# HGRN score levels in column strips, mLSTM products by head on array halves, and one conv tap moved to ScalarE

## The chip, the core and the metric

The kernel runs on one core of one Trainium2 chip. The metric is the device time of one execution in microseconds (us): the median of several runs. Beside these runs one execution is recorded by the hardware profiler; all rows of traces come from that one.

## What is computed

A decoder layer on 512 tokens of width 1024, in float32. Two half-step SwiGLU feed-forward blocks stand around a token mixer; each of the three has an RMS norm before and after it. The mixer has two groups of heads that read columns of one projection:

```python
# HGRN2, 4 heads of 128: S_t = diag(f_t) S_{t-1} + k_t v_t^T, o_t = S_t^T q_t
scores = jnp.sum(qc[:, :, :, None, :] * kc[:, :, None, :, :] * decay, axis=-1)   # decay = exp(G_t - G_s), s <= t
o = o_inter + jnp.einsum("bhts,bhsv->bhtv", scores, vc)
# mLSTM, 4 heads, q and k of 64, v of 128
num = inter[..., None] * jnp.einsum("bhtd,bhdv->bhtv", qc, C) + jnp.einsum("bhts,bhsv->bhtv", P, vc)
C_new = keep[..., None, None] * C + jnp.einsum("bhs,bhsd,bhsv->bhdv", w, kc, vc)
# q and k of the mLSTM go through a causal depthwise convolution of width 4
qk = jax.nn.silu(causal_depthwise_conv(jnp.concatenate([mq, mk], axis=-1), conv_w, conv_b))
```

## The kernel before

Everything lies in SBUF; weights stream from HBM. A weight tile is split into a high and a low float32r part (a copy on ScalarE, L208, and a subtraction on VectorE, L210), and a product is three matmuls: high by high, high by low, low by high. TensorE does these nearly all the time. The first feed-forward block comes first, the mixer's projections at L433 run from 364.4 us on, and after 600 us the second block follows. Inside the mixer the small products of the recurrences are plain float32; the trace shows each of these as two matmul records in a row on the same operands (112 matmuls at L1057 make 224 records).

**How the order is made.** Each engine runs its own program in order. The Tile framework places the instructions; the kernel steers TensorE by hand with `fill(n)`: the projections of the mixer (hq, conv, rows, hi, mv, hg, mo) wait in a queue of jobs cut into pieces, and `fill(n)` issues n pieces. A piece of hq or conv is 6 matmuls of 256 columns at L433; a piece of hi, mv, hg or mo is 3 of 512 columns (L126 to L128, called mm3 from here on). Stages of the recurrences stand between fills, so that TensorE works on projections while VectorE and ScalarE prepare the next stage. The four numbers in `FILL` are the pieces per step of the first HGRN pair of heads, the second pair, the mLSTM outputs and the HGRN outputs. The jobs are the same in number whatever FILL says; FILL moves them earlier or later.

**HGRN levels** (`hgrn_levels`, `hgrn_level`, `put`). The scores of a chunk of 128 tokens are built by levels. At level c a block of 2c tokens is halved; the first c tokens are keys, the second c are queries, and the decay goes by the boundary between them. VectorE forms the exponents (L1044, L1045), ScalarE takes exp (L1046, L1047), VectorE multiplies by q (L1049), TensorE forms the scores in one PSUM bank (L1057), and `put` copies the wanted blocks into `sT`. There are two passes (p = 0, 1), each for two heads, that is 8 tiles m of 128 keys by 64 queries, and the levels 64, 32, 16, 8, 4, 2. Before the change level 64 is 8 matmuls of 64 keys by 64 queries, level 32 is 16 of 32 by 32 in the key strips that begin at partitions 0 and 64, and levels 16 to 2 are 8 matmuls each of all 128 keys by 64 queries, from which `put` takes the valid parts with a mask on VectorE (L1030). The bursts of one level stand between fills of 6 pieces (p = 0) or 5 (p = 1). `ke` has two buffers.

**Convolution** (`conv`). ScalarE copies the projection out of PSUM (L1192), VectorE forms the last tap with the bias (L1195) and adds the three others (L1198), for four blocks, in the first pass of levels.

**mLSTM states** (`mlstm_scores`, L1287). For three chunks c and two pairs p of heads, one matmul makes keys (128 columns: two heads of 64) by values (258 columns: two heads of 129); only the two diagonal blocks are used (L1295, L1297). **mLSTM outputs** (`mlstm_values`). For each chunk and pair one bank takes query by state (L1332, 258 columns, from the second chunk on) and score by value for each head (L1335, 129 columns). ScalarE squares them (L1340), VectorE and GpSimd form the norm, and VectorE writes the scaled result (L1354), which frees the bank. `chunks` runs the three stages of four chunks in a staggered way with `fill(2)` between the steps. There are 8 PSUM banks.

Of the kernel before, what the change touches and what calls it, by code (L numbers as in the profile page):

```python
# [10 lines left out]
AF = mybir.ActivationFunctionType  # L11
ALU = mybir.AluOpType
PSUM = bass.MemoryType.PSUM

P = 128
# [8 lines left out]
PAIRS = NF // 2  # L24
HALF = T // 2
KH = ND // 2
FILL = (6, 5, 2, 2)
NH = 4
W = 512
HQ, HF, HI, HG, MQ, MV, MO, MG = 0, 512, 1024, 1536, 2048, 2560, 3072, 3584  # L30
# [37 lines left out]
class Layer:  # L68
# [950 lines left out]
    def put(self, p, n, sc):  # L1019

        c = LEVELS[n]
        so = self.sT[:, 8 * p : 8 * p + 8, :].rearrange("p n (b two c) -> p n b two c", two=2, c=c)[:, :, :, 1, :]
        if c >= 32:
            sc3 = sc.rearrange("p (n b c) -> p n b c", n=8, c=c)
            for b in range(64 // c):
                r = slice(2 * c * b, 2 * c * b + c)
                self.nc.scalar.copy(so[r, :, b], sc3[r, :, b])
            return
        mk = self.mask[:, n : n + 1, :].broadcast_to([P, 8, 64]).rearrange("p n (b c) -> p n b c", c=c)
        self.nc.vector.copy_predicated(so, mk, sc.rearrange("p (n b c) -> p n b c", n=8, c=c))  # L1030

    def hgrn_level(self, p, n, ke):

        nc = self.nc
        c = LEVELS[n]
        q, kk, G = self.q[p], self.kk[p], self.G[p]
        flat = lambda t: t.rearrange("p a t -> p (a t)")
        blk = lambda t: flat(t).rearrange("p (b two c) -> p b two c", two=2, c=c)
        qe = self.st("qe")
        qe3 = qe.rearrange("p (b c) -> p b c", c=c)  # L1040
        el = self.st("el")
        el3 = el.rearrange("p (b c) -> p b c", c=c)
        ref = blk(G)[:, :, 0, c - 1 : c].broadcast_to([P, 512 // c, c])
        nc.vector.tensor_tensor(qe3, blk(G)[:, :, 1, :], ref, op=ALU.subtract)  # L1044
        nc.vector.tensor_tensor(el3, ref, blk(kk)[:, :, 0, :], op=ALU.subtract)  # L1045
        nc.scalar.activation(qe, qe, AF.Exp)  # L1046
        nc.scalar.activation(blk(ke)[:, :, 0, :], el3, AF.Exp)  # L1047
        yield
        nc.vector.tensor_tensor(qe3, qe3, blk(q)[:, :, 1, :], op=ALU.mult)  # L1049
        yield  # L1050
        sc = self.ps()
        k8, q8 = flat(ke).rearrange("p (n s) -> p n s", s=P), qe.rearrange("p (n u) -> p n u", u=64)
        for m in range(8):
            for b in range(1 if c < 32 else 64 // c):
                r = slice(2 * c * b, 2 * c * b + c) if c >= 32 else slice(0, P)
                u = slice(c * b, c * b + c) if c >= 32 else slice(0, 64)
                nc.tensor.matmul(  # L1057
                    sc[r, 64 * m + u.start : 64 * m + u.stop], k8[:, m, r], q8[:, m, u], start=True, stop=True,
                    skip_group_check=True,
                )  # L1060
        yield
        self.put(p, n, sc)
        yield
# [124 lines left out]
    def conv(self, n, ps):  # L1188

        nc = self.nc  # L1190
        x = self.st("cx")
        nc.scalar.copy(x, ps)  # L1192
        tap = lambda j: self.prm[:, 4 * j + n : 4 * j + n + 1]
        y = self.qk[:, n, :]
        nc.vector.tensor_scalar(y, x, tap(3), self.prm[:, 16 + n : 17 + n], op0=ALU.mult, op1=ALU.add)  # L1195
        for j in range(3):
            s = 3 - j
            nc.vector.scalar_tensor_tensor(y[:, s:], x[:, : T - s], tap(j), y[:, s:], op0=ALU.mult, op1=ALU.add)  # L1198
# [30 lines left out]
    def mlstm_scores(self, mc):  # L1229

        nc = self.nc
# [52 lines left out]
        for c in range(3):  # L1284
            for p in range(2):
                ps = self.ps()
                nc.tensor.matmul(  # L1287
                    ps[:, :258], self.kw[:, p, c, :], self.vm[:, c, 2 * p : 2 * p + 2, :].rearrange("p a v -> p (a v)"),
                    start=True, stop=True,
                )  # L1290
                for a in range(2):
                    r = slice(64 * a, 64 * a + 64)
                    v = slice(129 * a, 129 * a + 129)
                    if c == 0:
                        nc.vector.tensor_copy(self.C[r, p, 0, v], ps[r, v])  # L1295
                    else:
                        nc.vector.scalar_tensor_tensor(  # L1297
                            self.C[r, p, c, v], self.C[r, p, c - 1, v], dcs[p][r, c - 1 : c], ps[r, v], op0=ALU.mult, op1=ALU.add
                        )
            self.fill(2)  # L1300
# [23 lines left out]
    def mlstm_values(self, c):  # L1324

        nc = self.nc
        s = slice(c * P, (c + 1) * P)
        pm = []
        for p in range(2):
            ps = self.ps()  # L1330
            if c:
                nc.tensor.matmul(ps[:, :258], self.qdm[:, p, (c - 1) * P : c * P], self.C[:, p, c - 1, :], start=True, stop=False)  # L1332
            for a in range(2):
                o = ps[:, 129 * a : 129 * a + 129]
                nc.tensor.matmul(o, self.pT[:, 2 * p + a, s], self.vm[:, c, 2 * p + a, :], start=c == 0, stop=c == 0 or a == 1)  # L1335
            pm.append(ps[:, :258].rearrange("p (a v) -> p a v", a=2))
        sq = self.sp.tile([P, 512], F32, tag="junk", bufs=1, name=self.nm("sq"))
        den, ab, ss, r = self.col(4), self.col(4), self.col(4), self.col(4)
        for p in range(2):
            nc.scalar.activation(sq[:, 256 * p : 256 * p + 256].rearrange("p (a v) -> p a v", a=2), pm[p][:, :, :P], AF.Square)  # L1340
        yield
        for p in range(2):
            nc.vector.tensor_copy(den[:, 2 * p : 2 * p + 2].rearrange("p (a o) -> p a o", o=1), pm[p][:, :, P : P + 1])
        nc.vector.tensor_reduce(ss, sq.rearrange("p (h v) -> p h v", h=4), axis=mybir.AxisListType.X, op=ALU.add)
        nc.vector.scalar_tensor_tensor(ab, den, -1.0, den, op0=ALU.mult, op1=ALU.max)
        nc.vector.tensor_tensor(ab, ab, self.emT[:, c, :], op=ALU.max)
        nc.vector.reciprocal(r, ab)
        nc.vector.tensor_tensor(ss, ss, r, op=ALU.mult)
        nc.vector.tensor_tensor(ss, ss, r, op=ALU.mult)
        f = self.rpow(ss, 1.0 / P, EPS)  # L1350
        nc.gpsimd.tensor_tensor(f, f, r, op=ALU.mult)
        yield
        for p in range(2):
            nc.vector.tensor_tensor(  # L1354
                self.y[:, c, W + 256 * p : W + 256 * p + 256].rearrange("p (a v) -> p a v", a=2),
                pm[p][:, :, :P],
                f[:, 2 * p : 2 * p + 2].rearrange("p (a o) -> p a o", o=1).broadcast_to([P, 2, P]),
                op=ALU.mult,
            )
        yield  # L1360
# [10 lines left out]
    def mixer(self):  # L1371
        nc, tc = self.nc, self.tc
        self.got, self.jobs = set(), deque()
        with tc.tile_pool(name="ma", bufs=1) as ma:
# [8 lines left out]
            with tc.tile_pool(name="mb", bufs=1) as mb:  # L1383
# [24 lines left out]
                for n in range(NH):  # L1408
                    nc.scalar.activation(self.q[n // 2][:, n % 2], qps[n], AF.Silu)
                self.hgrn_levels(0, kes, FILL[0])  # L1410
                self.until("rows")
                nc.scalar.activation(self.qk, self.qk, AF.Silu)
                self.hgrn_levels(1, kes, FILL[1], self.gate_rows(ma))
            with tc.tile_pool(name="mc", bufs=1) as mc:
# [5 lines left out]
                self.jobs.append(self.job_t("mo", self.gate_mo))  # L1420
                self.chunks(self.mlstm_values, FILL[2])
                self.until("hg")
                self.chunks(self.hgrn_values, FILL[3])
                self.until("mo")
# [128 lines left out]
```

## Time and profile before

| what | value |
|---|---|
| median of 3 runs | 952.54 us (952.47 to 953.07) |
| the profiled execution's own time | 953.22 us |
| its span, first to last instruction | 951.5 us |
| time around the span | 1.7 us |
| granted TensorE clock | 0.998 of full speed |

A timeline row gives the start (us from the span's start), the duration, the engine, the line, the operation, out<-in, and the shape: `128*32 128x32` is a matmul of 128 rows and 32 columns of the array whose output has 32 elements for each partition of the row's first number. `xN` is how many records are merged in the row; its duration runs from the first start to the last end. Matmuls overlap, since each begins before the one before has drained, so what a matmul takes away from the next is the distance of two starts. A row by groups gives the busy time of the group, the mean of one record in ns, and idle time before it. PE is TensorE's matmuls, DVE VectorE, ACT ScalarE, POOL GpSimd.

### The profile page before, as it was taken

The page shows a single profiled execution, that of the slowest core. Times are in us where ns is not written, and L with a number is a line of the kernel's source. Part 1 is how long each engine was busy: PE and PEld are TensorE (multiplying, and loading weights), DVE is VectorE, ACT ScalarE, POOL GpSimd, SP SyncE. Part 2 cuts the span into 40 slices and gives each one's busy share as a digit, 9 for nine tenths or more (in the row PEclk, how much of TensorE's full clock was granted, in tenths as well). Part 3 has the DMA queues.
Part 4 walks back from the last instruction along what each step waited for, and adds up shares of the span by engine and source line. Part 5 has one row for each costly group of instructions (what it writes and reads, how often), then busy time and mean ns, then how long its engine had stood idle before and what let it go on. Part 6 is the DMA issues. An engine that isn't in the chain of part 4 may idle for free.

```text
span 951.5 us, 15926 instructions
## 1 busy us (share of the span) xinstructions
PE 941.4 (99%) x6567; PEld 865.2 (91%) x6567; DVE 714.3 (75%) x798; ACT 466.1 (49%) x632; POOL 291.2 (31%) x225
## 2 busy tenths in 40 slices
PE   9999999999999999999999999999999999999997
PEld 7999999999888889998788888999999999988885
DVE  6798999998445376799856555797999999843543
ACT  7645454445344356966523345763445444533431
POOL 3546555751000036200010300354655565100001
PEclk9999999999999999999999999999999999999999
DMA  9243333325322014321312126214334332322202
GB/s 319 81 134 113 110 120 124 113 91 175 110 90 89 1 36 121 90 90 49 129 45 72 42 87 196 90 48 128 102 105 129 116 112 89 109 96 105 89 1 88
DMA packets 81666, 95.97 MB, mean 101 GB/s; under 512 B 4117, under 2 KB 61497, under 8 KB 81594
## 3 DMA queue, kind: packets, MB, share of 16 engines
q1 hardware_dynamic: 81306, 94.44, 31.0%
q8 instruction: 51, 0.84, 0.4%
q10 hardware_dynamic: 288, 0.52, 0.2%
q14 instruction: 21, 0.17, 0.1%
HBM read 92.85 MB, written 2.10 MB: 100 GB/s over the span
## 4 chain that ended last, share of the span: by engine, by line
PE 96%; DVE 2%; issue 1%; ACT 1%; DMA 0%; POOL 0%; DVEq 0%; POOLq 0%; ACTq 0%
PE ps L488 45%; PE ps L126 12%; PE ps L128 12%; PE ps L127 12%; PE ps L433 6%; PE ps L1057 2%; PE ps L267 2%; PE ps L443 1%; PE ps L115 0%; PE ps L1130 0%; PE ps L1335 0%; PE ps L1308 0%; PE ps L1332 0%; PE ps L1097 0%; PE ps L1310 0%
## 5 line engine op out<-in xcount | busy, mean ns | idle before, releaser
L210 DVE TENSOR_TENSOR w<-raw,w 128x1024 fp32r<-128x1024 f32 x214 | 363.0, 1704 | 123.1 <-ACT w L208 122.9
L208 ACT CAST w<-raw 128x1024 fp32r<-128x1024 f32 x214 | 224.0, 1053 | 314.6 <-PE ps L128 114.2
L222 POOL TENSOR_TENSOR raw<-raw,raw 128x1024 f32<-128x1024 f32 x80 | 221.0, 2764 | 170.8 <-DVE w L210 160.3
L488 PE MATMUL ps<-xq,w 128*128 128x256 f32 x2016 | 238.1, 277 | 0.0
L488 PEld LDWEIGHTS ps<-xq,w 128*128 128x128 f32 x2016 | 233.7, 188 | 0.2
L488 PE MATMUL ps<-sq,w 128*128 128x256 f32 x1440 | 171.0, 277 | 0.0
L488 PEld LDWEIGHTS ps<-sq,w 128*128 128x128 f32 x1440 | 167.4, 188 | 0.0
L128 PE MATMUL ps<-w,hs 128*128 128x512 f32 x336 | 131.0, 390 | 0.0
L126 PE MATMUL ps<-w,hs 128*128 128x512 f32 x336 | 130.9, 390 | 0.0
L127 PE MATMUL ps<-w,hs 128*128 128x512 f32 x336 | 130.8, 389 | 0.0
L126 PE MATMUL ps<-w,xq 128*128 128x512 f32 x208 | 84.7, 407 | 0.1
L128 PE MATMUL ps<-w,xq 128*128 128x512 f32 x208 | 81.1, 391 | 0.0
L127 PE MATMUL ps<-w,xq 128*128 128x512 f32 x208 | 81.1, 390 | 0.0
L128 PEld LDWEIGHTS ps<-w,hs 128*128 128x128 f32 x336 | 63.1, 188 | 13.8 <-DVE hs L672 0.7
L127 PEld LDWEIGHTS ps<-w,hs 128*128 128x128 f32 x336 | 63.1, 188 | 12.9
L126 PEld LDWEIGHTS ps<-w,hs 128*128 128x128 f32 x336 | 63.1, 188 | 12.8
L354 POOL TENSOR_SCALAR col<-col 128x1 f32<-128x1 f32 x24 | 9.5, 397 | 203.2 <-ACT junk L353 203.1
L433 PE MATMUL ps<-xq,w 128*128 128x256 f32 x480 | 55.7, 277 | 0.0
L433 PEld LDWEIGHTS ps<-xq,w 128*128 128x128 f32 x480 | 55.1, 188 | 0.1
L672 DVE TENSOR_TENSOR hs<-hf,hs 128x1024 fp32r<-128x1024 f32 x42 | 51.1, 1218 | 0.0
L128 PEld LDWEIGHTS ps<-w,xq 128*128 128x128 f32 x208 | 39.1, 188 | 8.9 <-DVE xq L274 0.3
L126 PEld LDWEIGHTS ps<-w,xq 128*128 128x128 f32 x208 | 39.1, 188 | 8.7 <-ACT xq L273 0.7
(241 smaller groups left out, 963.4 us busy)
## 6 DMA issues: line engine op xcount, KB each, us to landing
raw<-in_ffn_w_in_dram SPq DMA_DIRECT2D x88, 512.0 KB, 4.1
raw<-in_ffn_w_out_dram SPq DMA_DIRECT2D x44, 512.0 KB, 3.4
raw<-in_w_mix_in_dram SPq DMA_DIRECT2D x28, 512.0 KB, 3.7
raw<-in_w_mix_out_dram SPq DMA_DIRECT2D x8, 512.0 KB, 3.5
out_dram<-xs SPq DMA_DIRECT2D x8, 256.0 KB, 2.0
xs<-in_x_dram SPq DMA_DIRECT2D x6, 256.0 KB, 6.8
gpost<-in_norm_post_dram SPq DMA_DIRECT2D x3, 512.0 KB
gpre<-in_norm_pre_dram SPq DMA_DIRECT2D x2, 512.0 KB, 4.1
```

The costliest lines, as they stand in the source:

```text
L126: mm(ps, sh, mh, start=start, stop=False, **kw)
L127: mm(ps, sh, ml, start=False, stop=False, **kw)
L128: mm(ps, sl, mh, start=False, stop=stop, **kw)
L208: nc.scalar.copy(hi, raw)
L210: nc.vector.tensor_tensor(lo, raw, hi.bitcast(F32), op=ALU.subtract)
L222: nc.gpsimd.tensor_tensor(o, o, c, op=ALU.add)
L267: self.nc.tensor.transpose(pt[:, c * P : (c + 1) * P], src[:, k * P : (k + 1) * P], self.ident)
L433: mm(ps[:, u0:u1], w[:, a, k, :], self.xop(k, b, u0, u1), start=k + n + m == 0, stop=k == ND - 1 and n == 2, skip_group_check=True,)
L443: self.nc.tensor.matmul(ps[:, :HALF], w[:, a, k, :], self.xop(k, b, 0, HALF), start=m + k == 0, stop=m == 2 and k == ND - 1)
L488: self.nc.tensor.matmul(ps[:, c], wb[b][:, k, v], left[d][:, k, :], start=first and a + n + k == 0, stop=n == 2 and k == KH - 1, skip_grou ...
L672: self.nc.vector.tensor_tensor(t[:, 1], src, t[:, 0].bitcast(F32), op=ALU.subtract)
L1057: nc.tensor.matmul(sc[r, 64 * m + u.start : 64 * m + u.stop], k8[:, m, r], q8[:, m, u], start=True, stop=True, skip_group_check=True,)
```

## The change

1. `hgrn_level`: levels 64, 16, 8, 4, 2 are issued as strips of at most 32 keys. Level 64 takes two strips (partitions 0 and 32) of 32 keys by 64 queries; level 16 takes four strips (0, 32, 64, 96) of 16 keys by the 16 queries that belong to them; levels 8, 4 and 2 take four strips of 32 keys by all 64 queries. Level 32 stays. In matmuls per pass: level 64 from 8 to 16, levels 16, 8, 4, 2 from 8 to 32 each.
2. `put`: level 16 is copied by ScalarE in four copies of 16 partitions, and no longer by VectorE with the mask.
3. `FILL[0]` is 7 and no longer 6.
4. `conv`: the last tap with the bias is a ScalarE activation that reads PSUM.
5. mLSTM states: per chunk and pair two matmuls of 64 columns of the array by 129.
6. mLSTM outputs: the banks are by head of the pair (a) and no longer by pair (p). Query by state is one matmul for each head on 64 rows of the array, with the head's half of the rows; all four come first, into both banks, and then the four score products. Only the first matmul of a bank has the start flag.

```diff
-FILL = (6, 5, 2, 2)
+FILL = (7, 5, 2, 2)
...
-        if c >= 32:
+        if c >= 16:
...
+        r, u = {64: (32, 64), 32: (32, 32), 16: (16, 16)}.get(c, (32, 64))
+        blocks = [(0, 0), (32, 0)] if c == 64 else [(2 * c * b, b) for b in range(64 // c)] if c >= 16 else [(32 * b, 0) for b in range(4)]
         for m in range(8):
-            for b in range(1 if c < 32 else 64 // c):
-                r = slice(2 * c * b, 2 * c * b + c) if c >= 32 else slice(0, P)
-                u = slice(c * b, c * b + c) if c >= 32 else slice(0, 64)
+            for s0, b in blocks:
+                v = slice(64 * m + u * b, 64 * m + u * b + u)
                 nc.tensor.matmul(
-                    sc[r, 64 * m + u.start : 64 * m + u.stop], k8[:, m, r], q8[:, m, u], start=True, stop=True,
-                    skip_group_check=True,
+                    sc[s0 : s0 + r, v], k8[:, m, s0 : s0 + r], q8[:, m, u * b : u * b + u],
+                    start=True, stop=True, skip_group_check=True,
                 )
...
-        nc.vector.tensor_scalar(y, x, tap(3), self.prm[:, 16 + n : 17 + n], op0=ALU.mult, op1=ALU.add)
+        nc.scalar.activation(y, ps, AF.Identity, scale=tap(3), bias=self.prm[:, 16 + n : 17 + n])
...
-                nc.tensor.matmul(
-                    ps[:, :258], self.kw[:, p, c, :], self.vm[:, c, 2 * p : 2 * p + 2, :].rearrange("p a v -> p (a v)"),
-                    start=True, stop=True,
-                )
+                for a in range(2):
+                    r, v = slice(64 * a, 64 * a + 64), slice(129 * a, 129 * a + 129)
+                    nc.tensor.matmul(
+                        ps[r, v], self.kw[:, p, c, r], self.vm[:, c, 2 * p + a, :], start=True, stop=True, skip_group_check=True
+                    )
...
-        for p in range(2):
-            ps = self.ps()
-            if c:
-                nc.tensor.matmul(ps[:, :258], self.qdm[:, p, (c - 1) * P : c * P], self.C[:, p, c - 1, :], start=True, stop=False)
-            for a in range(2):
-                o = ps[:, 129 * a : 129 * a + 129]
-                nc.tensor.matmul(o, self.pT[:, 2 * p + a, s], self.vm[:, c, 2 * p + a, :], start=c == 0, stop=c == 0 or a == 1)
+        banks = [self.ps() for _ in range(2)]
+        if c:
+            for p in range(2):
+                for a in range(2):
+                    r = slice(64 * a, 64 * a + 64)
+                    nc.tensor.matmul(
+                        banks[a][:, 129 * p : 129 * p + 129], self.qdm[r, p, (c - 1) * P : c * P],
+                        self.C[r, p, c - 1, 129 * a : 129 * a + 129], start=p == 0, stop=False, skip_group_check=True,
+                    )
+        for a in range(2):
+            for p in range(2):
+                o = banks[a][:, 129 * p : 129 * p + 129]
+                nc.tensor.matmul(
+                    o, self.pT[:, 2 * p + a, s], self.vm[:, c, 2 * p + a, :], start=c == 0, stop=True, skip_group_check=True
+                )
```

The lines after these read the two banks by head: the squares, the copies of the denominators and the final products take strided halves of `sq`, `den`, `f` and `y`.

More of the change, by code (lines that the diff above doesn't have):

```diff
@@ L1327, in mlstm_values @@
         s = slice(c * P, (c + 1) * P)
-        pm = []
-        for p in range(2):
-            ps = self.ps()
-            if c:
-                nc.tensor.matmul(ps[:, :258], self.qdm[:, p, (c - 1) * P : c * P], self.C[:, p, c - 1, :], start=True, stop=False)
-            for a in range(2):
-                o = ps[:, 129 * a : 129 * a + 129]
-                nc.tensor.matmul(o, self.pT[:, 2 * p + a, s], self.vm[:, c, 2 * p + a, :], start=c == 0, stop=c == 0 or a == 1)
-            pm.append(ps[:, :258].rearrange("p (a v) -> p a v", a=2))
+        banks = [self.ps() for _ in range(2)]
[13 more added lines that the diff above has]
+                )
+        pm = [ps[:, :258].rearrange("p (q v) -> p q v", q=2) for ps in banks]
+        of = lambda t, a: t.rearrange("p (q a v) -> p a q v", q=2, a=2)[:, a]
         sq = self.sp.tile([P, 512], F32, tag="junk", bufs=1, name=self.nm("sq"))
@@ L1339, in mlstm_values @@
         for p in range(2):
-            nc.scalar.activation(sq[:, 256 * p : 256 * p + 256].rearrange("p (a v) -> p a v", a=2), pm[p][:, :, :P], AF.Square)
+            nc.scalar.activation(of(sq, p), pm[p][:, :, :P], AF.Square)
         yield
         for p in range(2):
-            nc.vector.tensor_copy(den[:, 2 * p : 2 * p + 2].rearrange("p (a o) -> p a o", o=1), pm[p][:, :, P : P + 1])
+            nc.vector.tensor_copy(of(den, p), pm[p][:, :, P : P + 1])
         nc.vector.tensor_reduce(ss, sq.rearrange("p (h v) -> p h v", h=4), axis=mybir.AxisListType.X, op=ALU.add)
@@ L1354, in mlstm_values @@
             nc.vector.tensor_tensor(
-                self.y[:, c, W + 256 * p : W + 256 * p + 256].rearrange("p (a v) -> p a v", a=2),
+                of(self.y[:, c, W:], p),
                 pm[p][:, :, :P],
-                f[:, 2 * p : 2 * p + 2].rearrange("p (a o) -> p a o", o=1).broadcast_to([P, 2, P]),
+                of(f, p).broadcast_to([P, 2, P]),
                 op=ALU.mult,
```

## The prediction, made before the changed kernel had run

> **What bounds the kernel now.** I read the page first, then the waits of TensorE, the busy time by stretches, and the timeline of the mixer, where all edits lie.
>
> ```profile
> span 951.5 us, 15926 instructions
> PE 941.4 (99%) x6567; PEld 865.2 (91%) x6567; DVE 714.3 (75%) x798; ACT 466.1 (49%) x632; POOL 291.2 (31%) x225
> ...
> PE 96%; DVE 2%; issue 1%; ACT 1%; DMA 0%; POOL 0%; DVEq 0%; POOLq 0%; ACTq 0%
> ```
> ```profile
> PE ps L1057 <- ACT ke L1047: 1.5, 1, 1.5
> ```
> ```profile
> 398.00:444.00 46.00, 46.00 (x385) 43.57 (x384) 43.17 (x60) 34.12 (x45) 0.00 (x0) 1.00 0.25 78
> 458.00:460.00 2.00, 0.52 (x6) 0.25 (x5) 2.00 (x4) 0.63 (x2) 0.00 (x0) 1.00 0.19 29
> ```
>
> TensorE is 99% busy and 96% of the chain that ended last. In the mixer it sits idle once, for 1.5 us, before the first level of the second pass. The columns of the last two rows are the stretch, its length, and the busy time of PE, PEld, DVE, ACT and POOL. From 398 to 444 us, the first pass of levels, VectorE works 43.17 of 46.00 us; around 459 us it works without a pause while TensorE waits. So the time is TensorE's stream plus one wait for VectorE. What an edit is worth is how much it takes out of the distance between one start and the next on TensorE.
>
> **The levels.** The trace holds each shape of burst; here are the second pass's level 32 and its level 16 with the neighbours.
>
> ```profile
> L1057 PE MATMUL ps<-qe,ke 128*128 128x64 f32 x128 | 15.1, 271 | 0.0
> L1057 PE MATMUL ps<-qe,ke 128*64 128x64 f32 x32 | 2.3, 224 | 1.5 <-ACT ke L1047 1.5
> L1057 PE MATMUL ps<-qe,ke 128*32 128x32 f32 x64 | 1.4, 197 | 0.0
> ```
> ```profile
> 459.78 1.12 PE L1057 MATMUL ps<-qe,ke 128*64 128x64 f32 x16 [1.48 <-ACT ke L1047]
> ...
> 465.53 0.39 PE L128 MATMUL ps<-w,xq 128*128 128x512 f32 x1
> 465.85 0.70 PE L1057 MATMUL ps<-qe,ke 128*32 128x32 f32 x32
> 466.48 0.50 PE L126 MATMUL ps<-w,xq 128*128 128x512 f32 x1
> ...
> 467.05 0.40 PE L128 MATMUL ps<-w,xq 128*128 128x512 f32 x1
> ...
> 469.79 0.39 PE L128 MATMUL ps<-w,xq 128*128 128x512 f32 x1
> 470.01 1.89 PE L1057 MATMUL ps<-qe,ke 128*128 128x64 f32 x16
> 471.71 0.48 PE L126 MATMUL ps<-w,xq 128*128 128x512 f32 x1
> ...
> 472.26 0.39 PE L128 MATMUL ps<-w,xq 128*128 128x512 f32 x1
> ```
>
> The plain stream: 12 mm3 records from 467.05 to 469.79, 0.228 us each. *Full width (levels 16 to 2 before)*: from 469.79 to 472.26 are 2.47 us, in which three mm3 records start (0.68), so a burst takes 1.79 us. Its starts spread over 1.89 - 0.27 = 1.62 us in 15 steps, 0.108 each. *Two strips (level 32)*: from 465.53 to 467.05, 1.52 - 0.68 = 0.84 us. Its 32 starts spread over 0.70 - 0.20 = 0.50 us, 0.016 each; the strips at 0 and 64 run side by side, so a pair takes 0.0325 and 16 pairs 0.52. The rest, 0.32, is going into the narrow shape and out again. *64 columns (level 64)*: 1.12 - 0.22 = 0.90 us in 15 steps, 0.060 each.
>
> *Levels 8, 4, 2 after*: 32 matmuls, 64 records, in four strips, each with 16 records of 64 queries. If the four run side by side, four records take what one record of level 64 takes, with the same 64 queries: 16 x 0.060 = 0.96, plus 0.32, is 1.28. Six such bursts: 6 x (1.79 - 1.28) = **-3.1 us**. Per record that is 0.015 us, about what level 32 shows with two strips, so it asks no faster issue; at 0.016 it would be 1.36, in all -2.6.
>
> *Level 16 after*: 64 records of 16 keys by 16 queries. The lower bound is four records in level 32's pair time, 0.52; the upper is level 32's distance for each record, 64 x 0.016 = 1.04. These are not far apart; I take 0.75 and keep both. 2 x (1.79 - 0.75 - 0.32) = **-1.4 us** (-0.9 to -1.9).
>
> *Level 64 after*: two strips, each with 16 records of 64 queries at 0.060: as before, **0**, if strips that touch (0 and 32) run side by side as 0 and 64 do. If not, +0.96 each.
>
> **The wait at 459.78.** It is put down to ScalarE; VectorE's rows show what was late.
>
> ```profile
> 426.57 0.73 DVE L1030 COPY_PREDICATED sT<-mask,ps 128x512 f32<-128x512 int32 x1
> ...
> 454.21 1.36 DVE L1012 COPY_PREDICATED sT<-eye,ps 128x512 f32<-128x512 int32 x2
> 456.06 1.33 DVE L1030 COPY_PREDICATED sT<-mask,ps 128x512 f32<-128x512 int32 x1
> 457.17 1.26 DVE L210 TENSOR_TENSOR w<-raw,w 128x1024 fp32r<-128x1024 f32 x1
> 458.94 0.69 DVE L1049 TENSOR_TENSOR qe<-qe,q 128x512 f32<-128x512 f32 x1
> ```
> ```profile
> L1195 DVE TENSOR_SCALAR qk<-cx,prm 128x512 f32<-128x512 f32 x4 | 2.1, 534 | 0.0
> ```
> ```profile
> L1192 ACT COPY cx<-ps 128x512 f32<-128x512 f32 x4 | 2.3, 582 | 0.0
> L1027 ACT COPY sT<-ps 32x256 f32<-32x256 f32 x2 | 0.7, 360 | 0.0
> ```
>
> The queries of that level come from L1049 at 458.94, ending 459.63; TensorE starts at 459.78. VectorE loses four taps (4 x 0.53) and level 16's masked copy (the row at 426.57): 2.8 us less ahead of this point. In the order of the changed program this L1049 also stands ahead of the two L1012, the L1030 and the L210 at 454.21 to 457.17, which is 4 us more (1.36 + 1.33 + 1.26). TensorE comes later: with FILL 7 it has 21 more mm3 records ahead of the burst (4.8 us) and saves about 2.2 in the first pass's bursts. All of it together is some 9 us against a wait of 1.48, so it goes: **-1.5 us**. What is late next is TensorE itself. ScalarE takes over four taps of about 0.58 and four copies per pass of at most 0.36, some 4 us on 34.12 of 46.00: still idle time. The steps of the first pass get longer on TensorE (6 to 7 pieces of three mm3 records, 0.68), so its other levels don't begin to wait; in the second pass each step loses 0.5 us, but there VectorE waits for TensorE. The moved pieces are only moved: 18 mm3 records fewer stand at the end of the mixer.
>
> **mLSTM.** One step of the states, one of the outputs, and the one place where the trace has 64-row products:
>
> ```profile
> 512.31 1.03 PE L1287 MATMUL ps<-vm,kw 128*128 128x258 f32 x4
> 513.00 0.58 PE L126 MATMUL ps<-w,xq 128*128 128x512 f32 x1
> ...
> 513.65 0.40 PE L128 MATMUL ps<-w,xq 128*128 128x512 f32 x1
> ```
> ```profile
> 521.36 0.60 PE L1332 MATMUL ps<-C,qdm 128*128 128x258 f32 x2
> 521.79 0.61 PE L1335 MATMUL ps<-vm,pT 128*128 128x129 f32 x4
> 522.23 0.60 PE L1332 MATMUL ps<-C,qdm 128*128 128x258 f32 x2
> ...
> 523.03 0.48 PE L126 MATMUL ps<-w,xq 128*128 128x512 f32 x1
> ...
> 523.58 0.40 PE L128 MATMUL ps<-w,xq 128*128 128x512 f32 x1
> ```
> ```profile
> 499.65 0.39 PE L128 MATMUL ps<-w,xq 128*128 128x512 f32 x1
> 499.96 1.16 PE L1223 MATMUL ps<-qk 64*128 64x128 f32 x16
> ...
> 501.85 0.40 PE L128 MATMUL ps<-w,xq 128*128 128x512 f32 x1
> ```
>
> States: 512.31 to 513.65 less two mm3 records is 0.88. After: two column halves side by side, four records each at 0.110 (the four of L1335, quoted next, take 0.44 from start to start of the groups), plus the 0.32 of the narrow shape: 0.76. Three steps: **-0.4**. Outputs: 521.36 to 523.58 less two records is 1.76, half of it state products. After, these are four pairs, 0.44, plus what 64-row products cost at L1223: 2.20 us between the two L128, less four stream records (0.91) and eight pairs (0.88), is 0.41. 0.85 for 0.88: **-0.1** for three chunks. The halving is eaten by the change of shape.
>
> Both banks are now needed at a chunk's start, and with the shifted jobs the four accumulators of mo are claimed after chunk 1. In the changed order the third of these takes chunk 1's first bank.
>
> ```profile
> 529.07 0.76 DVE L1354 TENSOR_TENSOR y<-ps,col 128x256 f32<-128x256 f32 x2 [1.22 <-POOL col L1351]
> ```
>
> Chunk 1's products began at 521.36 and its first bank came free at 529.45, 8.1 us later. TensorE will ask after two steps of 1.73 and six mm3 records (1.37) and chunk 3's 1.73: 7.9. Behind that matmul stands the whole stream. If nothing else shifts the wait is 0.2. In the changed order a weight split (L210, 1.26 above) stands ahead of chunk 1's chain on VectorE, so 1.5 at most; below, 0. I take **+0.4**, near the lower end, since VectorE had such a split in this stretch before as well.
>
> **Sum.** -3.1 - 1.4 - 1.5 - 0.4 - 0.1 + 0.4 = -6.1 us. The profiled execution took 953.22 us, the span and 1.7 around it that no edit touches; that is 0.68 over the median of 952.54. It would take 947.1, and the median **946.4 us**. With the ends of the terms the forecast itself reaches from -7.8 to -3.7: 944.7 to 948.8.
>
> **Rivals.** *The waits stay* (949.0): the 1.48 remains, since the order moved, and the banks cost 1.5: -6.1 + 1.5 + 1.1 = -3.5. Against it: 9 us of margin. *Strips that touch take turns* (slower): level 32 only ever used strips 0 and 64. If 0 and 32 share a way in, four strips make two turns: levels 8, 4, 2 take 32 x 0.060 + 0.32 = 2.24, +0.45 six times; level 16 32 x 0.0325 + 0.32 = 1.36, -0.43 twice; level 64 +0.96 twice. +2.7 - 0.9 + 1.9, and the rest -1.6: +2.1, 954.6 us. It decides from where four records of 64 queries take over 0.092 instead of 0.060. For it: no row has touching strips. Against it: each strip's loads and products already overlapped another's fully. *A floor for each record*: if a record costs a fixed time whatever the strip, 64 a burst lose from 0.023 us on.
>
> ```profile
> 461.63 0.22 PE L1173 MATMUL ps<-ident,z 4*128 4x4 f32 x1
> ...
> 462.09 0.20 PE L1174 MATMUL ps<-ident,z 4*128 4x4 f32 x1
> ```
>
> These eight tiny transposes come 0.066 apart; at that price a burst is 4.5 us and the kernel some 23 us slower. But level 32's 32 records at 0.016 speak against any floor above that. The Trainium skill, "TensorE: Matmul & The Clock Gate", section "Wait — 56ns, not 53.3ns?", says that starts never come closer than about 25 ns, however few columns. By that rule a burst is an estimated 1.92 us, +0.13 eight times, and the kernel stands at about 952; level 32's 0.016 disagrees with the rule across two strips, and no run here shows four.
>
> **Chances.** Forecast 0.70, waits stay 0.10, strips take turns 0.10, a floor 0.05, something unnamed 0.05. About 0.2% (1.9 us) is what a measurement of this kernel can tell from no change. Faster by more: 0.70 + 0.10 = 0.80. Within: the floor near its break-even and part of the turns, 0.10. Slower: 0.10. The range holds the forecast and the waits: 944.5 to 950.5.
>
> **What would show it.** Right: in levels 8, 4, 2 sixty-four records whose starts spread over 0.9 to 1.0 us; level 64 unchanged at 0.9; no idle before the second pass; about 1.76 for a chunk of outputs. Wrong: 1.9 us for those sixty-four (turns), a spread of level 64 near 1.9, the records of every level evenly more than 0.023 apart (floor), or idle PE rows at L126 behind chunk 3 that end with L1364 (banks).

## The result, and the profile after

The changed kernel takes **946.49 us**, the median of six runs (946.11 to 947.05), beside 952.75 (952.47 to 953.55) for the kernel before on the same chip: a ratio of 0.9933 with a 95% interval of 0.992 to 0.9946. The forecast was 946.4.

The profiled execution of after took 946.11 us, that of before 953.22: 7.1 less. Not all of that is the change. The next two fences show TensorE in the first microseconds, before then after. The code there is the same.

```profile
10.84 1.91 PE L267 MATMUL ps<-ident,hf 128*128 128x128 f32 x8
12.58 1.61 PE L488 MATMUL ps<-xq,sq 128*128 128x256 f32 x11
```
```profile
10.16 1.11 PE L267 MATMUL ps<-ident,hf 128*128 128x128 f32 x8
11.43 2.84 PE L488 MATMUL ps<-xq,sq 128*128 128x256 f32 x22 [0.17 <-ACT xq L287]
```

Eight transposes take 1.91 us in the one execution and 1.11 in the other, and L488 begins 1.15 us earlier. The distance then stays the same up to the mixer. So 7.11 - 1.15 = 5.96 us are from the change in the traces, and 952.75 - 946.49 = 6.26 by the medians.

The page of after, with the lines that answer to those of before; then TensorE's waits; then the two stretches (stretch, length, busy time of PE, PEld, DVE, ACT, POOL, granted clock, DMA share, GB/s); then the groups of the levels.

```profile
span 944.4 us, 16810 instructions
PE 934.9 (99%) x7007; PEld 853.4 (90%) x7007; DVE 713.4 (76%) x792; ACT 469.6 (50%) x644; POOL 290.6 (31%) x225
...
PE 85%; DVE 7%; ACT 3%; issue 2%; POOL 2%; DMA 0%; DVEq 0%; POOLq 0%; ACTq 0%
```
```profile
PE ps L128 <- DVE xq L274: 0.4, 1, 0.4
PE ps L126 <- DVE y L1364: 0.3, 1, 0.3
```
```profile
398.00:444.00 46.00, 46.00 (x599) 41.56 (x598) 41.41 (x55) 38.37 (x54) 0.00 (x0) 1.00 0.24 71
458.00:460.00 2.00, 2.00 (x20) 1.45 (x20) 2.00 (x3) 1.36 (x3) 0.00 (x0) 1.00 1.06 425
```
```profile
L1058 PE MATMUL ps<-qe,ke 128*32 128x64 f32 x448 | 8.8, 221 | 0.0
L1058 PE MATMUL ps<-qe,ke 128*32 128x32 f32 x64 | 1.4, 197 | 0.0
L1058 PE MATMUL ps<-qe,ke 128*16 128x16 f32 x128 | 1.4, 180 | 0.0
```

TensorE is still 99% busy. The wait of 1.5 us before the second pass is gone from the waits, and from 458 to 460 us TensorE now works without a pause. Two small waits are new. The chain's share of TensorE fell from 96% to 85%, which looks like a new bound and is none: such a short wait leads the walk back onto another engine, where it stays for a while. The matmul groups of the levels last 11.6 us together with 640 records instead of 18.8 with 224 (15.1 + 2.3 + 1.4).

The bursts themselves, in the timeline of after: first a weight load that waited at a bank, then level 64, level 16 and level 8 of the second pass, one step of the mLSTM states, one chunk of the outputs.

```profile
455.32 0.19 PEld L126 LDWEIGHTS ps<-w,xq 128*128 128x128 f32 x1 [0.53 <-ACT vh L1403]
...
459.67 1.09 PE L1058 MATMUL ps<-qe,ke 128*32 128x64 f32 x32
...
469.67 0.39 PE L128 MATMUL ps<-w,xq 128*128 128x512 f32 x1
469.99 0.69 PE L1058 MATMUL ps<-qe,ke 128*16 128x16 f32 x64
...
470.96 0.39 PE L127 MATMUL ps<-w,xq 128*128 128x512 f32 x1
...
473.93 0.39 PE L128 MATMUL ps<-w,xq 128*128 128x512 f32 x1
474.25 1.10 PE L1058 MATMUL ps<-qe,ke 128*32 128x64 f32 x64
...
475.61 0.40 PE L127 MATMUL ps<-w,xq 128*128 128x512 f32 x1
...
508.71 0.39 PE L128 MATMUL ps<-w,xq 128*128 128x512 f32 x1
509.03 0.66 PE L1290 MATMUL ps<-vm,kw 128*64 128x129 f32 x8
...
509.96 0.39 PE L127 MATMUL ps<-w,xq 128*128 128x512 f32 x1
...
517.53 0.40 PE L128 MATMUL ps<-w,xq 128*128 128x512 f32 x1
517.86 0.72 PE L1335 MATMUL ps<-C,qdm 64*128 64x129 f32 x8
518.50 1.16 PE L1342 MATMUL ps<-vm,pT 128*128 128x129 f32 x8
...
519.73 0.39 PE L127 MATMUL ps<-w,xq 128*128 128x512 f32 x1
```

A burst is the time from the stream record before it to the second one behind it, less two stream records of 0.227. Level 16: 470.96 - 469.67 - 0.45 = 0.83. Level 8: 475.61 - 473.93 - 0.45 = 1.23. States: 0.80. Outputs: 1.745. With the same sums for all bursts of the two traces:

| term | predicted | measured |
|---|---|---|
| levels 8, 4, 2 | -3.1 | 6 x (1.24 - 1.79) = -3.3 |
| level 16 | -1.4 | 2 x (0.83 - 1.79) = -1.9 |
| level 64 | 0 | -0.1 |
| wait before the second pass | -1.5 | -1.5 |
| states | -0.4 | 3 x (0.80 - 0.87) = -0.2 |
| outputs | -0.1 | 3 x (1.745 - 1.775) = -0.1 |
| bank waits in the outputs | +0.4 | 0.53 at chunk 3 (0.3 of it idle, the row of L126), less 0.29 that before had at chunk 2: +0.2 |
| the weight load at 455.32: a bank that ScalarE's L1403 frees late | not named | +0.4 |
| transposes of the mixer's output (the row of L128, 554 us) | not named | +0.4 |
| sum | -6.1 | -6.0 (added up before rounding) |

### The profile page after: what moved, and what is told of

The parts are those of the page before. It is cut to its first block, busy times and chain, and to the rows that moved or that the text cites. A ratio compares the mean times of both kernels' runs of the same rounds, so it can differ in the third digit from the quotient of the medians.

```text
span 944.4 us, 16810 instructions
## 1 busy us (share of the span) xinstructions
PE 934.9 (99%) x7007; PEld 853.4 (90%) x7007; DVE 713.4 (76%) x792; ACT 469.6 (50%) x644; POOL 290.6 (31%) x225
## 4 chain that ended last, share of the span: by engine, by line
PE 85%; DVE 7%; ACT 3%; issue 2%; POOL 2%; DMA 0%; DVEq 0%; POOLq 0%; ACTq 0%
PE ps L488 45%; PE ps L126 11%; PE ps L128 11%; PE ps L127 11%; PE ps L433 3%; DVE w L210 1%; PE ps L267 1%; POOL col L259 1%; DVE qk L1199 1%; PE ps L1058 1%; POOL col L354 0%; DVE el L1045 0%; DVE w L216 0%; ACT w L208 0%; PE ps L115 0%
## 5 line engine op out<-in xcount | busy, mean ns | idle before, releaser
L488 PE MATMUL ps<-xq,w 128*128 128x256 f32 x2016 | 238.1, 277 | 0.0
L488 PEld LDWEIGHTS ps<-xq,w 128*128 128x128 f32 x2016 | 233.7, 188 | 0.2
L488 PE MATMUL ps<-sq,w 128*128 128x256 f32 x1440 | 171.0, 277 | 0.0
L488 PEld LDWEIGHTS ps<-sq,w 128*128 128x128 f32 x1440 | 167.4, 188 | 0.0
L128 PE MATMUL ps<-w,hs 128*128 128x512 f32 x336 | 131.0, 390 | 0.0
L126 PE MATMUL ps<-w,hs 128*128 128x512 f32 x336 | 130.9, 390 | 0.0
L126 PE MATMUL ps<-w,xq 128*128 128x512 f32 x208 | 84.7, 407 | 0.5 <-DVE y L1364 0.3
L128 PE MATMUL ps<-w,xq 128*128 128x512 f32 x208 | 81.2, 392 | 0.4 <-DVE xq L274 0.4
L128 PEld LDWEIGHTS ps<-w,hs 128*128 128x128 f32 x336 | 63.1, 188 | 13.8 <-DVE hs L672 0.7
L126 PEld LDWEIGHTS ps<-w,hs 128*128 128x128 f32 x336 | 63.1, 188 | 12.8
L126 PEld LDWEIGHTS ps<-w,xq 128*128 128x128 f32 x208 | 39.1, 188 | 10.7 <-issue 1.4
L128 PEld LDWEIGHTS ps<-w,xq 128*128 128x128 f32 x208 | 39.0, 188 | 9.4 <-DVE xq L274 0.8
```

Source lines behind the costliest of these rows:

```text
L126: mm(ps, sh, mh, start=start, stop=False, **kw)
L128: mm(ps, sl, mh, start=False, stop=stop, **kw)
L488: self.nc.tensor.matmul(ps[:, c], wb[b][:, k, v], left[d][:, k, :], start=first and a + n + k == 0, stop=n == 2 and k == KH - 1, skip_grou ...
```

## The experiments: which part brings what

Each experiment is compared with the kernel before on the same chip (medians 952.63 to 952.90); 953.22 and 946.11 are not used here.

**Strips alone.** The kernel before, with the loops of `hgrn_level` and `if c >= 16` in `put` of the changed one.

> The kernel before with the strips of levels 64, 16, 8, 4, 2 alone, and level 16 copied by ScalarE; FILL stays 6, the tap stays on VectorE, mLSTM stays. Theory (the bursts are the gain, the wait before the second pass is TensorE ahead of VectorE): six bursts of 1.79 become 1.24 (-3.3), two become 0.83 (-1.9); TensorE comes 2.6 us earlier to the second pass's level 64, VectorE loses only one masked copy (0.73) ahead of it, so the wait of 1.5 grows to about 3.4. 952.75 - 5.2 + 1.9 = 949.4 us, with one idle row of 3 to 3.5 us at level 64 of the second pass. Rival (the wait goes with the strips by itself): 952.75 - 5.2 - 1.5 = 946.0.

950.98 us (950.30 to 952.86), ratio 0.9985 (0.9976 to 0.9994): only 1.8 of the 5.3 that the bursts save. The wait did grow, and something came that neither side had named. The stretches (columns as above; the granted clock is the third number from the end) and the row of the wait:

```profile
455.32 0.39 PE L128 MATMUL ps<-w,xq 128*128 128x512 f32 x1
458.86 0.40 PE L1058 MATMUL ps<-qe,ke 128*32 128x64 f32 x6 [3.15 <-DVE qe L1049]
```
```profile
459.00:462.00 3.00, 3.00 (x38) 2.54 (x34) 2.20 (x5) 2.66 (x5) 0.00 (x0) 0.51 0.61 180
462.00:465.00 3.00, 3.00 (x19) 2.58 (x19) 2.90 (x6) 2.26 (x5) 0.00 (x0) 0.92 0.22 31
```

After an idle time of 3.15 us the clock is at half for 3.4 us (459.04 to 462.46). In before the idle time of 1.48 left it at 1.00. The expected 949.4 lacked this price: the level-64 stretch takes 3.2 us more than before, not 1.9.

**FILL taken back.** The changed kernel with one number undone.

```diff
-FILL = (7, 5, 2, 2)
+FILL = (6, 5, 2, 2)
```

> The changed kernel with FILL[0] back at 6. Theory (FILL moves the wait away, by 4.8 us of stream before the second pass and by an order on VectorE in which the query product of level 64 stands ahead of the diagonal copies): in this kernel that product stands behind the two diagonal copies, the masked copy and a weight split again, so the wait comes back with 1.5 + 2.6 (shorter bursts) - 2.8 (four taps, one masked copy) = 1.3 us; the new waits of 0.38 at 455 us and 0.45 at 554 us may go. 946.5 + 1.3 - 0 to 0.8 = 947.0 to 947.8. Rival (VectorE's relief by the tap alone removes the wait): no idle row at level 64, 945.7 to 946.5.

**954.92 us** (953.76 to 955.91), ratio 1.0022 (1.0012 to 1.0031): both guesses are wrong by 7 us or more, and this kernel, with every shorter burst, is slower than before. Wait and clock:

```profile
455.78 0.39 PE L128 MATMUL ps<-w,xq 128*128 128x512 f32 x1
460.30 0.50 PE L1058 MATMUL ps<-qe,ke 128*32 128x64 f32 x5 [4.13 <-DVE qe L1049]
...
466.01 0.63 PE L126 MATMUL ps<-w,xq 128*128 128x512 f32 x1
466.44 0.63 PE L127 MATMUL ps<-w,xq 128*128 128x512 f32 x1
```
```profile
460.00:462.00 2.00, 1.70 (x32) 1.71 (x32) 2.00 (x5) 1.21 (x3) 0.00 (x0) 0.50 0.60 133
462.00:469.00 7.00, 7.00 (x30) 5.54 (x25) 3.93 (x7) 3.69 (x7) 0.00 (x0) 0.50 0.38 114
469.00:471.00 2.00, 2.00 (x30) 1.42 (x30) 0.00 (x0) 0.00 (x0) 0.00 (x0) 0.80 0.00 0
```

TensorE idles 4.13 us, and the clock is at 0.50 until shortly before 470: the stream's records start 0.43 apart instead of 0.227. From the last stream record before the wait until the stream has its pace again, this place takes 11.1 us beyond the stream's own time, where the changed kernel has 2.6. The wait is longer than in the kernel with strips alone, though VectorE has four taps less. The query product L1049, which ends the wait, starts 1.47 us later (459.49 for 458.02), while TensorE's last record before the wait is only 0.46 later (455.78 for 455.32). ScalarE's silu of the convolution shows where the 1.5 us come from; first strips alone, then this kernel:

```profile
429.97 1.28 ACT L1413 ACT_TABLE_LOAD   x1
433.34 1.92 ACT L1413 ACTIVATE qk<-qk 128x2048 f32<-128x2048 f32 x1 [2.09 <-DVE qk L1199]
```
```profile
433.55 1.28 ACT L1422 ACT_TABLE_LOAD   x1 [2.17 <-DVE qk L1199]
434.84 1.92 ACT L1422 ACTIVATE qk<-qk 128x2048 f32<-128x2048 f32 x1
```

Both wait for VectorE's last sum of the convolution. In the first kernel the table of the function is loaded (1.28 us) during that wait; in the second the load itself stands behind it, and what follows is 1.5 us late: VectorE then waits 2.58 us for ScalarE's L998, where strips alone has 0.24. The changed kernel and the next one, which differ by the tap alone, show the same: with the tap on ScalarE the load waits for VectorE (430.01, after 0.67 us idle), with the tap on VectorE it does not (430.78, directly behind L1138). That this costs 1.5 us with FILL at 6 is read from the traces; the tap was not taken back in this kernel.

**The tap taken back.** The changed kernel with L1196 as a VectorE `tensor_scalar` again.

> The changed kernel with the convolution's last tap back on VectorE. Theory (the margin of the wait is several us, so four taps of 0.53 do not matter): 946.5 within 0.4, no idle at level 64 of the second pass over 0.3 us. Rival (the tap is needed): the wait returns with up to 1.5 us, 947 to 948.

946.60 us (946.34 to 946.83), no wait at level 64: in this kernel the tap changes nothing that can be measured, in agreement with the theory. The query product of level 64 ends 5.2 us before its burst begins (454.93 and 460.12), so a late table load has room.

**FILL alone,** on the kernel before.

> The kernel before with FILL[0] = 7 and nothing else. Theory (FILL alone takes away the wait of 1.5 before the second pass, and brings back 0.4 at the transposes of the mixer's output and up to 0.4 at a bank of the second pass): 952.75 - 1.5 + 0.4 to 0.8 = 951.7 to 952.1. Rival 1 (strips are needed for that wait to go): 952.7. Rival 2 (the full 1.5 and no new wait): 951.2.

951.62 us (951.17 to 953.07), ratio 0.9989 (0.998 to 0.9997), and TensorE's waits:

```profile
PE ps L128 <- DVE xq L274: 0.3, 1, 0.3
...
PE ps L126 <- DVE y L1354: 0.2, 1, 0.2
```

The wait before the second pass is gone without any strip, and both small waits of the changed kernel are here: they are the price of moving pieces forward, since VectorE's work behind the mixer (L274) and the norm of the outputs (L1354) is late for a stream that lacks them.

**mLSTM alone,** on the kernel before.

> The kernel before with the mLSTM changes alone (states by head, outputs by head with each bank cleared once). Theory (the changes of shape eat the halving, and a bank wait of 0.2 to 0.3 more appears): states 3 x (0.80 - 0.87) = -0.2, outputs -0.05, banks +0.2: 952.7, not told from the kernel before. Rival 1 (the gain of 0.5 that the forecast had, with no bank wait): 952.2. Rival 2 (without the moved jobs the banks wait 1 us or more): 953.7.

953.35 us (952.87 to 954.11), ratio 1.0007 (0.9998 to 1.0015): not told from before, if anything 0.6 slower. The states show the 0.80 and the outputs the 1.75, but one chunk waits at its second bank:

```profile
524.16 0.49 PE L1334 MATMUL ps<-C,qdm 64*128 64x129 f32 x2
525.19 0.68 PE L1334 MATMUL ps<-C,qdm 64*128 64x129 f32 x6 [0.54 <-DVE y L1363]
```

Here the matmuls of both banks come first, so the second bank is needed by the third record of the chunk, where before first finished the other bank (0.87 us, from 521.36 to 522.23 in the prediction's rows), and VectorE's L1363 has not yet freed it. With this wait the chunk takes 2.73 us, where before took 2.07 at this chunk, a wait of 0.29 included.

By themselves strips, FILL and mLSTM bring -1.79 - 1.24 + 0.58 = -2.45 us; the tap was only taken back from the whole, where it is worth nothing. Together they bring -6.26. The difference of 3.8 is for the most part the 3.2 us that the longer wait and its clock cost the strips, and that FILL takes away.

## The experiments: how strips work

**Order.** The changed kernel with the two loops exchanged.

```diff
-        for m in range(8):
-            for s0, b in blocks:
+        for s0, b in blocks:
+            for m in range(8):
```

> The changed kernel with the two loops of a level's burst exchanged: all eight tiles of one strip, then the next strip. Same matmuls, same results. Theory (neighbours in the queue run side by side only if they use different strips, and a strip takes 0.058 us for a record of 64 queries and 0.0325 for one of 32 or 16): strips follow one another, 64 x 0.058 = 3.7 us of starts instead of 0.88 in levels 8, 4, 2 (+2.8 six times), 64 x 0.0325 = 2.1 instead of 0.52 at level 16 (+1.6 twice), 32 x 0.058 = 1.86 instead of 0.87 at level 64 (+1.0 twice), 1.04 instead of 0.50 at level 32 (+0.5 twice): +23, 969.5 us. Rival 1 (narrow matmuls are cheap in any order, strips have nothing to do with it): 946.5 and the same spreads. Rival 2 (each strip has a queue of its own deep enough to run ahead of the order): same spreads, 946.5 to 948.

962.89 us (962.64 to 963.03). A burst of level 8:

```profile
484.75 3.18 PE L1058 MATMUL ps<-qe,ke 128*32 128x64 f32 x64
```

Its starts spread over 2.96 us (3.18 less 0.22 of the last record), against 1.10 - 0.22 = 0.88 in the changed order. So the same 64 records run side by side only if neighbours in the order stand in different strips: 3.4 times faster. Both rivals are out. The size was too high: one strip alone takes 2.96 / 63 = 0.047 for a record, not 0.058, so side by side costs each strip a little. With the spreads of this trace (2.96 for 0.88 six times, 1.34 for 0.52, 1.56 for 0.87 and 0.90 for 0.50 twice each) the sum is 16.3 us; the kernel is 16.4 slower. The rule of the Trainium skill that the prediction weighed ("TensorE: Matmul & The Clock Gate", section "Wait — 56ns, not 53.3ns?"), no start within about 25 ns of another, holds within one strip here: at level 16 of this kernel, with 16 queries, the records of a strip start 0.025 apart (ten steps from 479.74 to 479.99). Across strips it does not hold (0.88 / 63 = 0.014, and 0.008 at level 16 of the changed kernel).

**Number of strips.** Levels 8, 4, 2 in two strips of 64 keys: half the matmuls.

```diff
-blocks = ... else [(32 * b, 0) for b in range(4)]
+blocks = ... else [(64 * b, 0) for b in range(2)]
```

> The changed kernel with levels 8, 4 and 2 in two strips of 64 keys (partitions 0 and 64) instead of four of 32: 32 records of 64 queries for each burst instead of 64. Theory (a strip takes 0.058 us for a record of 64 queries whatever its width, and strips run side by side): 16 pairs x 0.058 = 0.9, as with four strips; the burst stays 1.24 and the kernel 946.5. Rival 1 (the price is by record, 0.014 us): 32 x 0.014 = 0.45, burst 0.8, -0.44 six times, 943.9. Rival 2 (a wider strip is slower, as the full width with 0.108): 16 x 0.08 or more, burst 1.6 or more, 948.7.

946.86 us (946.43 to 946.96), and the row

```profile
474.44 1.15 PE L1058 MATMUL ps<-qe,ke 128*64 128x64 f32 x32
```

Half as many records take as long: the burst is 1.28 to 1.29, 0.05 more than with four strips. The price is by what each strip has to do, not by record. The gain of levels 8, 4, 2 comes from leaving the full width, and two strips would have done.

**Fewer queries.** Each strip of 32 keys needs only the 16 queries of its own tokens; the changed kernel multiplies by all 64 and masks.

```diff
-r, u = {...}.get(c, (32, 64))
+r, u = {...}.get(c, (32, 16))
-blocks = ... else [(32 * b, 0) for b in range(4)]
+blocks = ... else [(32 * b, b) for b in range(4)]
```

> The changed kernel, but levels 8, 4 and 2 multiply each strip of 32 keys by the 16 queries of the same 32 tokens alone (the others were computed and masked away), and VectorE copies the valid blocks in four masked copies of 32 partitions instead of one of 128. Same result. Theory (a strip's record costs 0.0325 us at 16 queries, as in level 16, and 0.058 at 64): bursts of 0.83 instead of 1.24, 6 x 0.41 = -2.4 us, if VectorE keeps up: 944.0. Rival (VectorE becomes late again: TensorE comes 1.2 us earlier to the second pass and the four copies cost VectorE more than the one of 0.7): an idle row at level 64 of the second pass of 0.5 to 2 us, 944.5 to 946.

945.96 us (945.75 to 946.30), ratio 0.9929 (0.9916 to 0.9941). The bursts are 0.87 (starts over 0.74 - 0.18 = 0.56), 6 x 0.37 = 2.2 less, and most of it is given back:

```profile
475.19 0.74 PE L1061 MATMUL ps<-qe,ke 128*32 128x16 f32 x64
```
```profile
PE ps L1061 <- ACT ke L1050: 1.0, 1, 1.0
PE ps L126 <- ACT vh L1406: 0.5, 1, 0.5
```

The wait of 1.0 is put down to ScalarE, but VectorE's order had moved back as well: the query product of this level, L1052, starts at 459.78, behind the diagonal copies as in before, where the changed kernel has it at 452.44. It ends 0.15 us before the burst starts at 460.61.

**A further piece.** The same with FILL[0] = 8.

> Levels 8, 4, 2 with their own 16 queries as before, and FILL[0] = 8. Theory (the shorter bursts of 0.87 are paid back as a wait of 1.0 at level 64 of the second pass and 0.5 at a bank that ScalarE empties, since TensorE comes earlier; 18 more moved products of the stream, 4.1 us, cover both): 946.0 - 1.5 = 944.5 us, no idle row at level 64. Rival (the pieces moved forward are missing behind the mixer, and the waits there, 0.4 at the transposes and 0.3 behind the mLSTM outputs, grow by as much): 945.5 to 946.

946.94 us (946.20 to 949.54). The theory fails, and the rival too: the wait at the second pass's level 64 is gone, but the queue of jobs is now empty before the last levels of that pass, which follow one another without a stream and wait there:

```profile
PE ps L1061 <- issue: 1.0, 1, 1.0
PE ps L1061 <- ACT ke L1050: 0.9, 1, 0.9
```

**Level 64 in four strips**, the second 32 queries in the strips at 64 and 96, with FILL[0] = 8 and own queries.

```diff
-blocks = [(0, 0), (32, 0)] if c == 64 else ...
+blocks = [(0, 0), (32, 0), (64, 1), (96, 1)] if c == 64 else ...
```

> The same with FILL[0] = 8, and level 64 in four strips: 32 keys by 32 queries each, the second half of the queries in the strips at 64 and 96, copied back by ScalarE to the partitions of the keys. 64 records instead of 32. Theory (a strip's record of 32 queries costs 0.0325, four strips run side by side): starts spread over 0.52 instead of 0.87, twice -0.35: 0.7 below the kernel with two strips, 943.8 if that one is at 944.5. Rival (strips that read the same keys hinder one another, or ScalarE's shifted copies are late): spread 0.87 or more, no gain.

944.32 us (944.10 to 944.79), ratio 0.9910 (0.9895 to 0.9925), the fastest of all. Level 64:

```profile
465.83 0.76 PE L1068 MATMUL ps<-qe,ke 128*32 128x32 f32 x64
```

Starts over 0.56 instead of 0.87; the stretch is 0.33 shorter in each pass, as expected. These 32 queries take as long as the 16 in the bursts of levels 8, 4, 2 above, also 64 records in four strips of 32 keys (0.56): with four strips in turn, what a strip takes falls from 64 to 32 queries, and below that no further. Of the rest of the 2.6 to the kernel just above, 0.5 is waits that fell otherwise (0.9 for 1.9 in the last levels, 1.0 for 0.5 at L1007); the remainder no trace shows, and the five runs of that kernel lie 3.3 apart.

**One more piece.**

> The same with FILL[0] = 9. Theory (with 8 nothing waits any more ahead of the second pass, so a further piece can only take work from behind the mixer): equal to FILL[0] = 8 or up to 0.5 slower. Rival (a wait is still left with 8): faster by that wait, up to 1 us.

948.29 us (947.82 to 949.02): 4.0 slower. The last levels of the second pass stand without a stream and wait for ScalarE and VectorE one after another (1.35, 0.60 and 1.78 us), and again the clock falls:

```profile
483.99 1.05 PE L1068 MATMUL ps<-qe,ke 128*32 128x16 f32 x64 [1.78 <-DVE qe L1058]
```
```profile
484.00:488.00 4.00, 4.00 (x75) 3.77 (x76) 3.46 (x9) 0.00 (x0) 0.86 (x1) 0.50 0.13 48
```

**Pieces spread anew.** FILL = (8, 4, 2, 2).

> The kernel with level 64 in four strips and levels 8, 4, 2 with their own queries, with FILL = (8, 4, 2, 2) instead of (8, 5, 2, 2). With 8 and 5 the queue of jobs is empty before the second pass's last two levels, whose bursts then wait 0.9 us for ScalarE with no stream between them. Theory (the stream only has to be spread: six pieces fewer in the second pass's first steps stand between its last bursts): the wait of 0.9 goes, the one of 1.0 ahead of the second pass's lowest level stays: 944.3 - 0.9 = 943.4 us. Rival (with steps of 4 pieces, 3.6 us, VectorE and ScalarE do not keep up in the second pass): the waits move to its first levels, 944.3 to 945.

944.42 us (943.67 to 944.79), ratio 0.9915 (0.9902 to 0.9929). In the trace the wait of 0.9 in the last levels is gone, as expected; the stretch of these levels is 0.5 shorter. The medians do not show it.

## Why the prediction was right, step by step

The forecast was the likeliest case, and the time came within 0.1 us of it. The sum held because errors cancelled, not because each term was exact.

- *What bounds the kernel*: right. TensorE's stream, so that a burst is worth its distance between starts.
- *Strips of levels 8, 4, 2*: right in mechanism and nearly in size (-3.3 for -3.1). The spread was 0.88, below the forecast's 0.9 to 1.0. Touching strips run side by side (levels 64 and 8, and the order exchanged as the counter-proof), so *strips take turns* is out, and *a floor for each record* too.
- *Level 16*: mis-sized. The value taken was 0.75 between bounds of 0.52 and 1.04; the spread is 0.52, the lower bound. Records of 16 queries in four strips take no longer than those of 32 queries in two at level 32.
- *The wait at 459.78*: its disappearance was right, its reasons were pooled too loosely. The sum of 9 us mixed VectorE's relief (2.8), an order on VectorE (4) and the moved stream (4.8 less 2.2). The size was near: from before to after the query product of level 64 moves 5.4 us ahead (458.94 to 452.44, less the 1.1 by which all of after is early there), where 2.8 + 4 were expected, and TensorE's last stream record ahead of the burst 2.6 back (457.91 to 459.35), as expected; 6.5 us of margin are left. The runs separate the causes in part: the tap is worth nothing in the changed kernel, FILL alone removes the wait, and without FILL the strips lengthen it from 1.5 to 3.2 or 4.1 us. FILL moves both the order on VectorE and the stream, and these two were not separated.
- *What it costs if the cover is gone*: this is what the prediction lacked. It priced *the waits stay* at 949.0. The kernel with the wait is at 954.9, for a longer wait halves the clock behind it. The risk on the slow side was this, more than strips that take turns.
- *The ends of the forecast*: -7.8 and -3.7 do not follow from the ends of its terms, which add up to -7.0 (-3.1, -1.9, -1.5, -0.4, -0.1, 0) and -4.0 (-2.6, -0.9, -1.5, -0.4, -0.1, +1.5). The measured change lies inside either.
- *"The moved pieces are only moved"*: the traces show 120 instead of 99 such records ahead of the second pass, so 21 and not 18 fewer behind it. And wrong by 0.4, the wait at the transposes behind the mixer, which FILL alone shows too.
- *mLSTM*: the halving is eaten by the change of shape, as forecast, a little more than forecast (states -0.2 for -0.4). *Bank waits*: the place behind chunk 3 and the releaser L1364 were right, 0.30 in the trace; the net is less, since before already waited 0.29 at another chunk.

## What to carry to other kernels

Split narrow products into column strips and let neighbours in the order alternate between strips; what a strip takes goes by its queries from 64 down to 32 (0.88 to 0.56 us here, and still 0.56 at 16), so cut the queries to 32 before cutting the keys further. When bursts get shorter, look first at where TensorE will overtake VectorE and ScalarE, and move independent stream there, but no more than the later stages can lack: the same strips gave 946.5 with 7 pieces and 954.9 with 6, and with still shorter bursts 8 and 9 pieces gave 944.3 and 948.3. Test the parts of a change alone: here the tap (taken back from the whole) and mLSTM brought nothing, and strips and FILL brought 3 us one by one, where the whole brought 6.

## What the runs showed of the hardware

**The clock falls behind idle time.** 1.48 us idle in before and 1.0 in the kernel with fewer queries left the granted clock at 1.00. Behind 3.15 us it was at half for 3.4 us. Behind 4.13 us it was at half for 10.2 us (459.54 to 469.78), and TensorE was busy from 460.30 on. With FILL[0] = 9 no idle stretch was longer than 1.78 us, but TensorE worked only 1.3 of the 4 us from 479 to 483, and the clock was at half for 6.8 us (482.79 to 489.62). So a few short waits in a row can be enough, and the three lengths are one, three and two times 3.4 us. In the kernel with strips alone eight of eleven executions took 950.3 to 951.2 us with a mean granted clock of 0.997, and three 952.5 to 952.9 with 0.993 to 0.995. The Trainium skill, "TensorE: Matmul & The Clock Gate", section "What's actually happening", says that the clock halves after an idle window of about 3.4 us, that the windows run freely, and that it is released after about 3.4 us of work. The traces agree in the unit of 3.4 us, and the runs in that the loss varies. They differ in two points: with FILL[0] = 9 the clock fell without an idle stretch near that length, and the return after 4.13 us idle came only after 9.5 us of work.

**Side by side has a measured size.** 64 records of 64 queries in four strips: 2.96 us strip after strip, 0.88 alternating. 16 or 32 queries instead of 64: 0.56 at 32 keys; 16 queries at 16 keys: 0.52. Going into strips of 32 or 16 columns and out again costs 0.31 (level 16) to 0.36 us (level 8) beyond that, now over a third of level 16's burst.
